# The first four steps of each attention group left to the scheduler, with half a fill tile emitted behind each of them

## The chip, the cores and the metric

The kernel runs on one core of a Trainium2 chip. The metric is device time in microseconds (us) of one execution; several runs of the same kernel are taken and their median is shown. One more execution was recorded by the hardware profiler, and all rows below come from that one.

## The reference, cut to what matters

One layer of a model with width 1024 and 1024 tokens. A projection of x is split into the operands of three branches (sparse attention, spatial gating, mLSTM), and their outputs are gated, merged and normalised. The change touches two places of it: the attention branch, and the projections whose results gate two of the branches.

```python
def query_block(qb):                      # 8 blocks of 128 queries, per group of 4 heads
    s_sel = einsum(q_blk, k_g) - slopes * d_sel       # selected blocks of keys
    p_sel = _masked_softmax(s_sel, m_sel)
    o_sel = einsum(p_sel, v_g)
    s_w = einsum(q_blk, k_w) - slopes * d_w           # window of 256 keys
    p_w = _masked_softmax(s_w, m_w)
    o_w = einsum(p_w, v_w)
o = gates[0] * o_cmp + gates[1] * o_sel + gates[2] * o_win
y_a = o * silu(a_z)
y_b = (gelu(b_u) * mixed) * silu(b_z)
```

## The kernel before, in words

Operands of matmuls are fp32, split into a high and a low part (type fp32r), so that one product is made of three matmuls: `proj_half` (L121) issues 24 matmuls of 128x512 for half a projected tile (8 pieces of the contraction, three products each). A weight tile comes by DMA (`wraw`), ScalarE writes its high part (L90) and VectorE its low part (L91).

Attention works on two groups g of four heads (`attend`, L611). `prep_group` (L359) projects keys and queries into the operands KA/KB and QA/QB. Then come nine steps. Step s does three things for query block s: the row maxima of its window scores (`ps_w`, L487) and selected scores (`ps_s`, L495) in `attn_max`, one VectorE reduction per head and 512 columns (L408, L411), a transpose of these maxima (`ps_m`, L502) and their write into QB (L503). For block s-1 it runs the `Back` object: scores again with the maximum folded into the operand (`ps_st`, L529 and L530), the exponential on ScalarE (L532), the product with V (`ps_o`, L557), four operations on VectorE that add each branch to `o` (L564 to L568), and `finish`, which transposes `o` (`ps_ot`, L574) and copies it into `ya`. For block s+1 it starts the compressed branch, `attn_cmp` (`ps_c` L425, softmax on VectorE and ScalarE, `ps_t` L461, `ps_co` L471).

Each matmul output lies in a bank of PSUM, taken in turn from a pool by name: two banks each for the projections ("pj"), for the scores ("st"), for the small outputs of the maxima and the compressed branch ("m") and for `ps_o`/`ps_ot` ("o").

The order of TensorE within a group is written out by hand: all of `attend` stands inside `tc.manual_schedule(engines={PE})`, so the matmuls of attention keep the order of the text. The other engines' orders are made by the scheduler from the dependences and its own modelled times.

Work that does not depend on attention stands behind it in the text: the fill tiles. `fill_bu` (L592) projects half a tile, then applies GELU into `yb` (its last operation is L173); `fill_bz` (L600) projects half a tile and multiplies `yb` with its SiLU; `fill_az` (L581) does the same for `ya`. Each half is one call of `proj_half` (24 matmuls, L127, output `ps_pj`). The scheduler slips these matmuls between those of attention where it models a wait there. Behind `attend(0)` stand bu and bz of 0 to 2, behind `attend(1)` bu and bz of 3 and az of 0 to 3.

A line number of the kernel after is one higher than before up to L588 (L574 before is L575 after).

Of the kernel before, what the change touches and what calls it, by code (L numbers as in the profile page):

```python
# [2 lines left out]

# [1 line left out]

# [17 lines left out]
NT = T // P  # L23
# [5 lines left out]
HPG = 4  # L29
# [14 lines left out]
def hybrid_kernel(ctx, tc, xm, pT, wfm, wvg, wtm, cmpw1, cmpw2, cpos, vecs, sgwT, sgb,  # L44
# [21 lines left out]
    def pst(tag, bufs, name=None):  # L66
        return ps.tile([P, 512], F32, tag=tag, bufs=bufs, name=name or f"ps_{tag}")

    def pj():
        return pst("pj", 2)  # L70
# [94 lines left out]
    def gelu2(dst, src, n):  # L165

        sq = tp.tile([P, 512], F32, tag="ge_a", bufs=2, name="ge_a")[:, :n]
        if len(src.shape) == 3:
            sq = sq.rearrange("p (a b) -> p a b", a=src.shape[1])
        act(sq, src, AF.Square, scale=GK)  # L170
        stt(out=sq, in0=sq, scalar=1.0, in1=src, op0=OP.add, op1=OP.mult)
        act(sq, sq, AF.Tanh, scale=GC)
        stt(out=dst, in0=sq, scalar=1.0, in1=src, op0=OP.add, op1=OP.mult)  # L173
# [10 lines left out]
    def wf(i, parts=1):  # L184
        return load_w(wfm[i], KT, P, parts)
# [72 lines left out]
    for m in range(4):  # L258
        for r, half in ((0, 0), (0, 1), (1, 0), (1, 1)) if m == 0 else ((0, 0), (1, 0), (0, 1), (1, 1)):
            k = 2 * m + r  # L260
# [52 lines left out]
    for kv in range(2):  # L313
        st = stk[kv]
        ph = pst("m", 2)
        for v in range(2):
            zb = yp.tile([P, T], F32, tag="y", bufs=YB, name="zb")
            z4 = zb[:, 0:1008].rearrange("p (j g n) -> p j g n", j=8, g=2)
            for j in range(8):
                i = 16 * v + 2 * j  # L320
# [40 lines left out]
    def prep_group(g):  # L361
        d = {}
        d["KAs"] = pk.tile([P, T], F32R, tag="KAs", bufs=1, name="KAs")
        d["KBs"] = pk.tile([P, T], F32R, tag="KBs", bufs=1, name="KBs")
        d["KAw"] = pk.tile([P, T], F32R, tag="KAw", bufs=1, name="KAw")
        d["KBw"] = pk.tile([P, T], F32R, tag="KBw", bufs=1, name="KBw")
        for n in "sw":
            vv.tensor_scalar_mul(d["KB" + n][64:128, 0:1], xls[3][1][64:128, 0:1].bitcast(F32), 0.0)
        nc.gpsimd.dma_start(out=d["KBs"][64:128, :], in_=augk[0])
        nc.gpsimd.dma_start(out=d["KBw"][64:128, :], in_=augk[1])  # L370
        w = wf(FM["kw"] + g)
        for half in range(2):
            po = pj()
            proj_half(po, w, half, xh, xl)
            s = slice(half * 512, half * 512 + 512)
            for j, n in enumerate(("s", "w")):
                src = po[j * 64:j * 64 + 64, :]
                A, B = d["KA" + n], d["KB" + n]
                nc.scalar.copy(A[0:64, s], src)
                nc.scalar.copy(B[0:64, s], src)  # L380
                vv.tensor_sub(A[64:128, s], src, B[0:64, s].bitcast(F32))
        QA, QB = [], []
        for hf in range(4):
            qa = pa2.tile([P, 2, HPG, P], F32R, tag="QA", bufs=4, name="QA")
            qb = pa2.tile([P, 2, HPG, P], F32R, tag="QB", bufs=4, name="QB")
            nc.gpsimd.dma_start(out=qb[64:128, :, :, :], in_=augq[g, hf])
            QA.append(qa)
            QB.append(qb)
        for pr in range(2):
            w = wf(FM["q"] + 2 * g + pr)  # L390
            for half in range(2):
                po = pj()
                proj_half(po, w, half, xh, xl)
                for a in range(2):
                    h = 2 * pr + a
                    for b in range(2):
                        src = po[a * 64:a * 64 + 64, b * 256:b * 256 + 256].rearrange("p (b q) -> p b q", b=2)
                        qh = QB[2 * half + b][0:64, :, h, :]
                        nc.scalar.mul(qh, src, 0.125)
                        nc.scalar.mul(QA[2 * half + b][64:128, :, h, :], src, 0.125)  # L400
                        stt(out=QA[2 * half + b][0:64, :, h, :], in0=src, scalar=0.125, in1=qh.bitcast(F32),  # L401
                            op0=OP.mult, op1=OP.subtract)
        d["QA"], d["QB"] = QA, QB
        return d
# [73 lines left out]
    def attn_max(g, qb, d):  # L478

        QB = d["QB"][qb // 2][:, qb % 2]  # L480
        mx = pa2.tile([P, 8], F32, tag="mx", bufs=3, name="mx")
        mx2 = pa2.tile([P, 4], F32, tag="mx2", bufs=3, name="mx2")
        j0 = max(0, qb - 2)
        nw = (qb - j0 + 1) * P
        for h in range(HPG):
            pw = pst("m", 2, "ps_w")
            mm(pw[:, 0:nw], lhsT=QB[:, h, :], rhs=d["KBw"][:, j0 * P:j0 * P + nw], start=True, stop=True)  # L487
            rowmax(mx[:, 4 + h:5 + h], pw, nw, winm[:, 384 - nw:384] if qb >= 2 else zrow[:, 512 - nw:512])
            yield
        ns = (qb + 1) * P  # L490
        for h in range(HPG):
            for c0 in range(0, ns, 512):
                n = min(512, ns - c0)
                pw = pst("m", 2, "ps_s")
                mm(pw[:, 0:n], lhsT=QB[:, h, :], rhs=d["KBs"][:, c0:c0 + n], start=True, stop=True)  # L495
                dst = mx if c0 == 0 else mx2
                rowmax(dst[:, h:h + 1], pw, n, zrow[:, 512 - n:512] if c0 + n == ns else None)
                yield
        if ns > 512:
            vv.tensor_max(mx[:, 0:4], mx[:, 0:4], mx2)  # L500
        pm = pst("m", 2, "ps_m")
        nc.tensor.transpose(pm[0:8, 0:P], mx, ident)  # L502
        vv.tensor_tensor(out=QB[96:104, :, :], in0=pm[0:8, 0:P].unsqueeze(1).to_broadcast([8, 4, P]),  # L503
                         in1=nblk.unsqueeze(2).to_broadcast([8, 4, P]), op=OP.mult)
# [76 lines left out]
    def fill_az(i):  # L581
        w = wf(FM["az"] + i)
        for half in range(2):
            po = pj()
            proj_half(po, w, half, xh, xl)
            y = ya[i][:, half * 512:half * 512 + 512]
            z = tp.tile([P, 512], F32, tag="ge_a", bufs=2, name="zz")
            act(z, po, AF.Tanh, scale=0.5)  # L588
            stt(out=z, in0=z, scalar=1.0, in1=po, op0=OP.add, op1=OP.mult)
            stt(out=y, in0=z, scalar=0.5, in1=y, op0=OP.mult, op1=OP.mult)  # L590

    def fill_bu(i):  # L592
        w = wf(FM["bu"] + i)
        for half in range(2):
            po = pj()
            proj_half(po, w, half, xh, xl)
            gelu2(yb[i][:, half * 512:half * 512 + 512], po, 512)

    def fill_bz(i):
        w = wf(FM["bz"] + i)  # L600
        for half in range(2):
            po = pj()
            proj_half(po, w, half, xh, xl)
            z = tp.tile([P, 512], F32, tag="ge_a", bufs=2, name="zz")
            silu2(z, po, 512, z)
            y = yb[i][:, half * 512:half * 512 + 512]
            vv.tensor_mul(y, y, z)

    def attend(g):  # L611
        with tc.manual_schedule(engines={mybir.EngineType.PE}):
            d = prep_group(g)
            cmp_ = attn_cmp(g, 0, d)
            next(cmp_)
            next(cmp_)
            for step in range(NT + 1):
                back = Back(g, step - 1, d) if step else None
                mxs = attn_max(g, step, d) if step < NT else iter(())
                nmx = (4 + HPG * (1 + step // 4)) if step < NT else 0  # L620
                last = back.n if back else 2
                done = 0
                for k in range(last + 1):
                    upto = nmx * (k + 1) // (last + 1)
                    mid = (done + upto + 1) // 2
                    for _ in range(done, mid):
                        next(mxs)
                    if back and k < back.n:
                        back.scores(k)
                    for _ in range(mid, upto):  # L630
                        next(mxs)
                    done = upto
                    if k == 0:
                        if step < NT:
                            next(cmp_)
                        cmp_ = attn_cmp(g, step + 1, d) if step + 1 < NT else iter(())
                        next(cmp_, None)
                    if back and k:
                        back.values(k - 1)
                if back:  # L640
                    back.finish()
                next(mxs, None)
                next(cmp_, None)
    attend(0)
    for i in range(3):
        fill_bu(i)
        fill_bz(i)
    attend(1)
    fill_bu(3)
    fill_bz(3)  # L650
    for i in range(4):
        fill_az(i)
    if "ya" in dbg:
        for i in range(4):
            nc.sync.dma_start(dbg["ya"][i], ya[i])
# [478 lines left out]
    for tt in range(NT):  # L1134
# [5 lines left out]
        for c in range(npc):  # L1140
            s = slice(c * n, c * n + n)
            pe = pst("m" if tt == 1 else "o", 2, "ps_e")
            i = 0
# [28 lines left out]
        last = tt == NT - 1  # L1172
# [118 lines left out]
```

## Time and profile before

| | us |
|---|---|
| median of 3 runs | 1372.73 |
| lowest and highest of them | 1371.12, 1374.52 |
| the profiled execution | 1371.17 |
| its span in the trace | 1369.1 |
| TensorE busy | 1337.7 (98%) |
| VectorE busy | 844.4 (62%) |
| ScalarE busy | 526.1 (38%) |
| GpSimd busy | 152.8 (11%) |

The span runs from the first to the last instruction that the profiler saw; the profiled execution's own time has 2.1 us around it and lies 1.6 us below the median. PE is TensorE, DVE VectorE, ACT ScalarE, POOL GpSimd. A row of the timeline gives the start and the duration of an instruction (or of a few merged ones, with their count), and in brackets the idle time of the engine just before it with what ended it. Matmuls are pipelined, so that the start-to-start distance, not the duration, is what a matmul takes of the engine.

### The profile page before, as it was taken

To read this page: it belongs to the slowest core of one execution; us is meant where nothing else is said; L and a number is where in the kernel's file an instruction comes from. 1 tells how busy PE (TensorE), PEld (TensorE's weight loads), DVE (VectorE), ACT (ScalarE), POOL (GpSimd) and SP (SyncE) were. 2 spreads that over 40 slices of the span, in tenths; PEclk is the share of its full clock that TensorE was granted. 3 is DMA by queue.
4 is the path that set the end of the run, shared out by engine and by line. 5 is a ranking of instruction groups with operands and counts; after the bars stand their busy time and mean duration, and the time that the engine had idled before them with its cause. 6 is when DMAs were issued, how large, how long until landed. Compare 5 with 4: busy or idle time off the path is not lost.

```text
span 1369.1 us, 18928 instructions
## 1 busy us (share of the span) xinstructions
PE 1337.7 (98%) x7135; PEld 1130.5 (83%) x7135; DVE 844.4 (62%) x1991; ACT 526.1 (38%) x1059; POOL 152.8 (11%) x173
## 2 busy tenths in 40 slices
PE   8998999998999999999999999999999999999997
PEld 6986888886888899988888888888878887888786
DVE  6247777336777467647776678766544555334855
ACT  6354333344333343135455355553442212324211
POOL 0012211101120100001001000010000444000312
PEclk9999999999999999999999999999999999999999
DMA  9131001111002141333223332236346543114201
GB/s 316 32 71 50 24 28 28 38 48 43 9 24 69 41 155 54 132 108 124 82 73 108 108 110 79 81 120 212 108 169 208 194 152 108 47 62 126 105 32 47
DMA packets 48059, 127.46 MB, mean 93 GB/s; under 512 B 5208, under 2 KB 16344, under 8 KB 47968
## 3 DMA queue, kind: packets, MB, share of 16 engines
q1 hardware_dynamic: 47008, 123.11, 27.4%
q0 software_dynamic: 960, 3.15, 1.1%
q8 instruction: 56, 0.92, 0.3%
q14 instruction: 35, 0.29, 0.1%
HBM read 101.00 MB, written 25.23 MB: 92 GB/s over the span
## 4 chain that ended last, share of the span: by engine, by line
PE 90%; DVE 5%; ACT 2%; DMA 2%; issue 1%; SPq 0%; POOL 0%; DVEq 0%; ACTq 0%; POOLq 0%
PE ps_pj L127 19%; PE ps_a L837 14%; PE ps_b L127 9%; PE ps_b L837 8%; PE ps_o L557 7%; PE ps_g L1106 5%; PE ps_st L148 3%; PE ps_pj L148 3%; PE ps_c L837 3%; PE ps_st L529 2%; PE ps_st L530 2%; PE ps_v L136 2%; PE ps_e L1146 2%; PE ps_s L495 1%; PE ps_w L487 1%
## 5 line engine op out<-in xcount | busy, mean ns | idle before, releaser
L127 PE MATMUL ps_pj<-xh,whi 128*128 128x512 f32 x288 | 115.5, 401 | 2.3 <-DVE QA L401 2.3
L127 PE MATMUL ps_pj<-xh,wlo 128*128 128x512 f32 x288 | 115.2, 400 | 0.0
L127 PE MATMUL ps_pj<-xl,whi 128*128 128x512 f32 x288 | 114.6, 398 | 0.0
L557 PEld LDWEIGHTS ps_o<-V,pt 128*128 128x128 f32 x912 | 110.2, 191 | 3.4
L557 PE MATMUL ps_o<-V,pt 128*128 128x65 f32 x912 | 108.3, 271 | 0.0
L532 ACT ACTIVATE pt<-ps_st 128x512 f32<-128x512 f32 x114 | 62.8, 596 | 89.3 <-PE ps_st L530 88.6
L837 PE MATMUL ps_a<-op_lo,sh 128*128 128x512 f32 x240 | 94.1, 392 | 0.0
L837 PE MATMUL ps_a<-op_hi,sl 128*128 128x512 f32 x240 | 93.8, 391 | 0.0
L837 PE MATMUL ps_a<-op_hi,sh 128*128 128x512 f32 x240 | 93.8, 391 | 0.0
L824 DVE TENSOR_TENSOR sl<-ss,sh 128x512 fp32r<-128x512 f32 x80 | 54.8, 690 | 59.0 <-ACT sh L823 58.9
L90 ACT CAST whi<-wraw 128x1024 fp32r<-128x1024 f32 x46 | 48.3, 1049 | 94.8 <-PE ps_b L127 44.7
L127 PE MATMUL ps_b<-sp_hi,wlo 128*128 128x512 f32 x192 | 74.8, 390 | 1.3 <-DVE wlo L91 1.3
L127 PE MATMUL ps_b<-sp_lo,whi 128*128 128x512 f32 x192 | 74.7, 389 | 0.0
L91 DVE TENSOR_TENSOR wlo<-wraw,whi 128x1024 fp32r<-128x1024 f32 x46 | 62.3, 1353 | 19.7 <-ACT whi L90 15.5
L127 PE MATMUL ps_b<-sp_hi,whi 128*128 128x512 f32 x192 | 73.9, 389 | 0.0
L1065 POOL TENSOR_TENSOR M<-M,gt 128x512 f32<-128x512 f32 x32 | 43.8, 1378 | 199.1 <-DVE gt L1064 183.5
L127 PEld LDWEIGHTS ps_pj<-xh,whi 128*128 128x128 f32 x288 | 54.3, 188 | 13.7 <-PE ps_pj L127 3.9
L127 PEld LDWEIGHTS ps_pj<-xh,wlo 128*128 128x128 f32 x288 | 54.3, 188 | 10.0
L127 PEld LDWEIGHTS ps_pj<-xl,whi 128*128 128x128 f32 x288 | 54.3, 189 | 9.3
L823 ACT CAST sh<-mraw 128x512 fp32r<-128x512 f32 x60 | 37.4, 623 | 57.1 <-PE ps_a L837 30.8
L823 ACT CAST sh<-ss 128x512 fp32r<-128x512 f32 x80 | 49.6, 620 | 22.9 <-PE ps_b L837 22.1
L824 DVE TENSOR_TENSOR sl<-mraw,sh 128x512 fp32r<-128x512 f32 x60 | 43.6, 727 | 22.8 <-ACT sh L823 22.8
(369 smaller groups left out, 3534.2 us busy)
## 6 DMA issues: line engine op xcount, KB each, us to landing
mraw<-in_wfm_dram SPq DMA_DIRECT2D x40, 512.0 KB, 3.6
gsc<-gt SPq DMA_DIRECT2D x24, 512.0 KB, 2.6
gt<-gsc SPq DMA_DIRECT2D x24, 512.0 KB, 4.3
wraw<-in_wfm_dram SPq DMA_DIRECT2D x18, 512.0 KB, 3.5
xraw<-in_xm_dram SPq DMA_DIRECT2D x14, 512.0 KB, 5.5
yraw<-ysc SPq DMA_DIRECT2D x12, 512.0 KB, 3.4
wraw<-in_wbr_dram SPq DMA_DIRECT2D x12, 512.0 KB, 5.0
wraw<-in_wtm_dram SPq DMA_DIRECT2D x8, 512.0 KB, 4.0
```

The lines of the kernel that those rows point to most:

```text
L90: nc.scalar.copy(hi[:, c], raw[:, c])
L91: vv.tensor_sub(lo[:, c], raw[:, c], hi[:, c])
L127: mm(po[:M, :], lhsT=a[:, k, :], rhs=b(k, half), start=(i == 0), stop=(i == n - 1))
L136: mm(po[:, :n], lhsT=tok(a, k, tt), rhs=b[:, k % 4, :], start=(i == 0), stop=(i == tot - 1))
L148: mm(po, lhsT=tok(a, 4 * i + k, tt), rhs=b[:, k, :], start=(i == 0 and tt % 2 == 0 and k == 0 and j == 0), stop=(i == 1 and k == 3 and j = ...
L532: act(pt.rearrange("p h q -> p (h q)"), sp, AF.Exp)
L557: mm(po[:, h * 65:h * 65 + 65], lhsT=pt[:, h, :], rhs=V[:, j, vi, :], start=(first and h == 0), stop=last, skip_group_check=True)
L823: nc.scalar.copy(hi, src)
L824: vv.tensor_sub(lo, src, hi)
L837: mm(bank, lhsT=l[a][:, k, :], rhs=r[b], start=first and k == 0 and i == 0, stop=k == K - 1 and i == 2, skip_group_check=True)
L1065: nc.gpsimd.tensor_add(M[n][:, s], M[n][:, s], t[:, s])
L1106: mm(po[:, 0:n], lhsT=a[k][:, ts_], rhs=b[k][:, s], start=(k == 0 and i == 0), stop=(k == KT - 1 and i == 2))
```

## The change

`FREE = 4`: `prep_group` and steps 0 to 3 of each group stand outside `manual_schedule`, so that the scheduler orders their matmuls on TensorE too; steps 4 to 8 stay inside. The three fill functions become generators that yield after each half, and one half is emitted behind each free step: bu0 and bz0 in group 0, bu3 and bz3 in group 1. The other fills stand behind the groups as before. No operation is added or taken away.

```diff
     def fill_bu(i):
         w = wf(FM["bu"] + i)
...
             proj_half(po, w, half, xh, xl)
             gelu2(yb[i][:, half * 512:half * 512 + 512], po, 512)
+            yield
...
-    def attend(g):
+    FREE = 4
+
+    def attend(g, fills):
+        d = prep_group(g)
+        cmp_ = attn_cmp(g, 0, d)
+        next(cmp_)
+        next(cmp_)
+
+        def one(step):
+            nonlocal cmp_
...
+        for step in range(FREE):
+            one(step)
+            next(fills, None)
         with tc.manual_schedule(engines={mybir.EngineType.PE}):
-            d = prep_group(g)
...
+            for step in range(FREE, NT + 1):
+                one(step)
+
+    attend(0, chain(fill_bu(0), fill_bz(0)))
+    for _ in chain(fill_bu(1), fill_bz(1), fill_bu(2), fill_bz(2)):
+        pass
+    attend(1, chain(fill_bu(3), fill_bz(3)))
+    for _ in chain(*(fill_az(i) for i in range(4))):
+        pass
-    attend(0)
-    for i in range(3):
-        fill_bu(i)
-        fill_bz(i)
-    attend(1)
-    fill_bu(3)
-    fill_bz(3)
-    for i in range(4):
-        fill_az(i)
```

The body of `one(step)` is that of the loop before, word for word. What it does to the order is seen where step 1 of group 0 ends and step 2 begins. On TensorE, before, the last `ps_o` of block 0 is followed at once by the transposes of `o` (here `q_1095` and `kbd_201` are numbered buffers of the compressed branch):

```order
L425 MATMUL ps_c<-kbd_201,q_1095 128x128 x2
L127 MATMUL ps_pj<-xl,whi 128x512
L495 MATMUL ps_s<-KBs,QB 128x256 x4
L557 MATMUL ps_o<-V,pt 128x65 x8
L574 MATMUL ps_ot<-ident,o 128x128 x2
L502 MATMUL ps_m<-ident,mx 8x128
L461 MATMUL ps_t<-ident,pcm 128x128 x2
L487 MATMUL ps_w<-KBw,QB 128x384
```

After the change the same place on TensorE begins so (the last `ps_o` is the fourth row):

```order
L472 MATMUL ps_co<-vbd_203,pts 128x128 x2
L426 MATMUL ps_c<-kbd_201,q_1129 128x128 x2
L558 MATMUL ps_o<-V,pt 128x65 x2
L496 MATMUL ps_s<-KBs,QB 128x256
L558 MATMUL ps_o<-V,pt 128x65 x6
L530 MATMUL ps_st<-QA,KAw 128x512
L496 MATMUL ps_s<-KBs,QB 128x256
L530 MATMUL ps_st<-QA,KAw 128x512
L496 MATMUL ps_s<-KBs,QB 128x256
```

and after fifteen matmuls of a fill tile, the last `ps_s` and the transpose `ps_m`, goes on with:

```order
L462 MATMUL ps_t<-ident,pcm 128x128 x2
L128 MATMUL ps_pj<-xh,whi 128x512
L128 MATMUL ps_pj<-xh,wlo 128x512
L128 MATMUL ps_pj<-xl,whi 128x512
L488 MATMUL ps_w<-KBw,QB 128x384
L128 MATMUL ps_pj<-xh,whi 128x512
L531 MATMUL ps_st<-QB,KBw 128x512 x2
L575 MATMUL ps_ot<-ident,o 128x128
L488 MATMUL ps_w<-KBw,QB 128x384
```

The transposes `ps_ot` have moved behind 19 matmuls of a fill tile and behind the first `ps_w` of step 2; two `ps_st` of step 2 that need no maximum (those with QA) have moved ahead.

On VectorE, before, the same place reads (the low part of a weight stands between the two branches of `o`):

```order
L436 TENSOR_TENSOR pcm<-pcm,sm 128x256
L568 SCALAR_TENSOR_TENSOR o<-ps_o,osc,o 128x64 x4
L566 TENSOR_TENSOR osc<-osc,gates 128x4
L91 TENSOR_TENSOR wlo<-wraw,whi 128x1024
L568 SCALAR_TENSOR_TENSOR o<-ps_o,osc,o 128x64 x4
L503 TENSOR_TENSOR QB<-ps_m,nblk 8x512
L173 SCALAR_TENSOR_TENSOR yb<-ge_a,ps_pj 128x512
```

After, a `yb` of a fill stands ahead of it (six rows higher than the first row here), the write of QB ahead of the second branch of `o`, and `wlo` behind two row maxima:

```order
L569 SCALAR_TENSOR_TENSOR o<-ps_o,osc,o 128x64 x2
L567 TENSOR_TENSOR osc<-osc,gates 128x4
L504 TENSOR_TENSOR QB<-ps_m,nblk 8x512
L569 SCALAR_TENSOR_TENSOR o<-ps_o,osc,o 128x64 x4
L412 ISA junk,mx<-ps_w,cr 128x384
L412 ISA mx 128x1
L578 COPY ya<-ps_ot 128x128
L412 ISA junk,mx<-ps_w,cr 128x384
L412 ISA mx 128x1
L92 TENSOR_TENSOR wlo<-wraw,whi 128x1024
```

Over the attention of each group, TensorE passes 74 times from an fp32 matmul (transposes, `ps_o`, `ps_c`, `ps_co`) to an fp32r one, before it did so 66 times. From the free steps' end on, the order on TensorE is that of before.

## Rows read from the trace of the kernel before

**Rows 1.** The page, part 1: busy time of each engine, with share and instructions.

```profile
PE 1337.7 (98%) x7135; PEld 1130.5 (83%) x7135; DVE 844.4 (62%) x1991; ACT 526.1 (38%) x1059; POOL 152.8 (11%) x173
```

**Rows 2.** Windows: stretch and length in us, busy PE, PEld, DVE, ACT, POOL; PEclk, DMA, GB/s.

```profile
98.00:120.00 22.00, 20.63 (x109) 15.83 (x107) 15.35 (x57) 12.76 (x42) 5.61 (x8) 1.00 0.16 43
120.00:128.00 8.00, 4.40 (x18) 3.29 (x17) 6.25 (x24) 2.08 (x6) 0.00 (x0) 0.57 0.23 66
128.00:304.00 176.00, 175.93 (x1038) 151.14 (x1037) 106.03 (x343) 64.46 (x152) 24.29 (x38) 1.00 0.11 32
334.20:342.20 8.00, 4.40 (x17) 3.28 (x17) 6.28 (x24) 2.02 (x6) 0.00 (x0) 0.61 0.20 67
342.20:593.00 250.80, 250.80 (x1756) 229.77 (x1756) 165.67 (x491) 82.86 (x169) 21.95 (x34) 1.00 0.22 70
```

**Rows 3.** Waits of PE, 90 to 180 us: waited for; total, times, longest in us.

```profile
PE ps_ot L574 <- DVE o L568: 3.3, 1, 3.3
PE ps_pj L127 <- DVE QA L401: 1.2, 2, 0.6
PE ps_s L495 <- DVE mx L411: 0.6, 2, 0.3
```

**Rows 4.** Timeline of PE, group 0, end of step 1.

```profile
118.57 1.90 PE L557 MATMUL ps_o<-V,pt 128*128 128x65 f32 x16
123.71 0.77 PE L574 MATMUL ps_ot<-ident,o 128*128 128x128 f32 x2 [3.25 <-DVE o L568]
...
125.47 0.69 PE L487 MATMUL ps_w<-KBw,QB 128*128 128x384 f32 x1 [0.35 <-DVE QB L503]
...
127.66 0.39 PE L487 MATMUL ps_w<-KBw,QB 128*128 128x384 f32 x1
```

**Rows 5.** Timeline of DVE, the same place.

```profile
121.12 0.85 DVE L568 SCALAR_TENSOR_TENSOR o<-ps_o,osc,o 128x64 f32<-128x64 f32 x4
...
121.96 1.22 DVE L91 TENSOR_TENSOR wlo<-wraw,whi 128x1024 fp32r<-128x1024 f32 x1
123.10 0.85 DVE L568 SCALAR_TENSOR_TENSOR o<-ps_o,osc,o 128x64 f32<-128x64 f32 x4
124.73 0.68 DVE L503 TENSOR_TENSOR QB<-ps_m,nblk 8x512 fp32r<-8x512 f32 x1 [0.78 <-PE ps_m L502]
125.45 0.69 DVE L173 SCALAR_TENSOR_TENSOR yb<-ge_a,ps_pj 128x512 f32<-128x512 f32 x1
```

**Rows 6.** Timeline of PE, group 1, the same place.

```profile
337.93 0.77 PE L574 MATMUL ps_ot<-ident,o 128*128 128x128 f32 x2 [3.25 <-DVE o L568]
...
341.88 0.52 PE L487 MATMUL ps_w<-KBw,QB 128*128 128x384 f32 x1
...
342.85 0.48 PE L127 MATMUL ps_pj<-xh,whi 128*128 128x512 f32 x1
```

**Rows 7.** Timeline of PE, group 0, later steps: the same work without a wait.

```profile
140.55 0.44 PE L487 MATMUL ps_w<-KBw,QB 128*128 128x384 f32 x1
...
141.75 0.33 PE L487 MATMUL ps_w<-KBw,QB 128*128 128x384 f32 x1
...
142.29 0.47 PE L127 MATMUL ps_pj<-xl,whi 128*128 128x512 f32 x1
...
157.19 0.27 PE L574 MATMUL ps_ot<-ident,o 128*128 128x128 f32 x1
157.30 0.27 PE L502 MATMUL ps_m<-ident,mx 128*8 128x128 f32 x1
...
157.55 0.48 PE L127 MATMUL ps_pj<-xh,whi 128*128 128x512 f32 x1
```

**Rows 8.** Timeline of PE: three fill matmuls behind a ps_o, the first one wider spaced.

```profile
136.14 0.48 PE L127 MATMUL ps_pj<-xh,wlo 128*128 128x512 f32 x1
136.46 0.39 PE L127 MATMUL ps_pj<-xl,whi 128*128 128x512 f32 x1
136.69 0.40 PE L127 MATMUL ps_pj<-xh,whi 128*128 128x512 f32 x1
```

More of the change, by code (lines that the diff above doesn't have):

```diff
@@ L2 @@
 from contextlib import ExitStack
+from itertools import chain
 import numpy as np
@@ L597, in fill_bu @@
             gelu2(yb[i][:, half * 512:half * 512 + 512], po, 512)
+            yield
     def fill_bz(i):
@@ L607, in fill_bz @@
             vv.tensor_mul(y, y, z)
-    def attend(g):
-        with tc.manual_schedule(engines={mybir.EngineType.PE}):
-            d = prep_group(g)
[L614 to L643, printed above, removed]
@@ L644, in hybrid_kernel @@
-    attend(0)
-    for i in range(3):
-        fill_bu(i)
-        fill_bz(i)
-    attend(1)
-    fill_bu(3)
-    fill_bz(3)
-    for i in range(4):
-        fill_az(i)
+            yield
+    FREE = 4
[6 more added lines that the diff above has]
+            nonlocal cmp_
+            back = Back(g, step - 1, d) if step else None
+            mxs = attn_max(g, step, d) if step < NT else iter(())
+            nmx = (4 + HPG * (1 + step // 4)) if step < NT else 0
+            last = back.n if back else 2
+            done = 0
+            for k in range(last + 1):
+                upto = nmx * (k + 1) // (last + 1)
+                mid = (done + upto + 1) // 2
+                for _ in range(done, mid):
+                    next(mxs)
+                if back and k < back.n:
+                    back.scores(k)
+                for _ in range(mid, upto):
+                    next(mxs)
+                done = upto
+                if k == 0:
+                    if step < NT:
+                        next(cmp_)
+                    cmp_ = attn_cmp(g, step + 1, d) if step + 1 < NT else iter(())
+                    next(cmp_, None)
+                if back and k:
+                    back.values(k - 1)
+            if back:
+                back.finish()
+            next(mxs, None)
+            next(cmp_, None)
+        for step in range(FREE):
+            one(step)
+            next(fills, None)
+        with tc.manual_schedule(engines={mybir.EngineType.PE}):
+            for step in range(FREE, NT + 1):
+                one(step)
```

## The prediction

> **What bounds the kernel now.** I read the page's first part before anything else: TensorE (PE) is busy for 98% of the span, the next engine (VectorE, DVE) for 62% [rows 1]. So a change in order can win only where PE is idle or runs at a low clock, and I look for those places with the windows over the two attention groups. The reader is to see two kinds of stretch there [rows 2]. From 128 to 304 us PE is busy for 175.93 of 176 us, from 342.2 to 593 us for all of 250.8, both at a granted clock of 1.00: nothing to win. From 120 to 128 us and from 334.2 to 342.2 us it is busy for 4.40 of 8 us, and the granted clock is 0.57 and 0.61, between the two levels of 1.00 (2.4 GHz) and 0.5 (1.2 GHz). Ahead of the first of these, from 98 to 120 us, lie 22.00 - 20.63 = 1.37 us of idle time at clock 1.00, in short pieces.
>
> The list of what PE waits for names the cause [rows 3]: one wait of 3.3 us of the transposes `ps_ot` for `o`, two of 0.6 us for QA, two of 0.3 us for a row maximum. The timelines show how the long one comes about [rows 4, 5]. The last `ps_o` of block 0 ends at 118.57 + 1.90 = 120.47 us. DVE then does the first branch of `o` (0.85 us), a weight's low part (1.22 us) and the second branch (0.85 us), which is done at 123.95 us. All that time PE has the transposes at the head of its hand-made order and can't pass them. Then the maxima are transposed, DVE writes QB (0.68 us), and the first `ps_w` of step 2 starts at 125.47 us. What follows is at half speed: from that `ps_w` over four `ps_st` to the next it takes 127.66 - 125.47 = 2.19 us, and the same six matmuls in a later step 141.75 - 140.55 = 1.20 us [rows 4, 7]. Group 1 has the same wait of 3.25 us in the same place [rows 6].
>
> **The change, part by part.**
>
> *The hole is filled.* After the change 19 fill matmuls, `ps_t` and two `ps_st` stand between the last `ps_o` and the transposes. A fill matmul takes 136.69 - 136.46 = 0.23 us from start to start [rows 8], so 19 are 4.4 us: about as long as DVE needs for `o` and QB. The stretch from 120.47 to 125.47 us, 5.00 us, holds useful work that takes little at full clock: 157.30 - 157.19 = 0.11 us for each of the two `ps_ot`, and 157.55 - 157.30 = 0.25 for `ps_m` and the two `ps_t` behind it [rows 7], together 0.47. What can be won is 5.00 - 0.47 = 4.53 us in each group. Nothing is made shorter by this: 19 fill matmuls that stood later now stand here, and since PE is full from 128 us on, the whole rest moves forward by as much.
>
> *The clock.* If PE doesn't stop, it doesn't fall to the lower level, and 2.19 - 1.20 = 0.99 us are won per group [rows 4, 7]. In group 1 the slow stretch goes on a little: from the second `ps_w` to the first fill matmul 342.85 - 341.88 = 0.97 us, against 142.29 - 141.75 = 0.54 [rows 6, 7], 0.43 more. Hole and clock together: 2 x (4.53 + 0.99) + 0.43 = 11.5 us. By the Trainium skill, "TensorE: Matmul & The Clock Gate", section "Terms", a stretch at the lower level costs its length times one minus the level's share of the full clock; a mean of 0.57 over 8 us would then cost 3.4 us a group in place of my 0.99, and the gain would be some 5 us larger. The trace speaks for the smaller figure, since most of the slow stretch was idle and only 18 matmuls stood in it.
>
> *The short waits.* In step 0 two `ps_st` that need no maximum move ahead, and fill matmuls are free to stand between `ps_s`. I count one of the two waits for QA (half of 1.2) and one of the two for a maximum (half of 0.6) as gone [rows 3]: 0.9 us a group, 1.8 in all. The first wait for QA, in `prep_group`, stays, as no filler is ready.
>
> *More changes of operand type.* In each group 8 more fp32r matmuls follow an fp32 one. The first fill matmul behind `ps_o` takes 136.46 - 136.14 = 0.32 us to the next start, those behind it 0.23 [rows 8]: 0.09 us each, so 2 x 8 x 0.09 = 1.4 us lost, all of it on PE and so on the path.
>
> *New short waits.* The fill halves bring their own work for DVE and ScalarE into steps 1 to 3: `yb` (0.69 us), a weight's low part (1.22 us) [rows 5]. DVE was busy for 15.35 of 22 us from 98 to 120 us [rows 2], and with two or three more such operations in each step it comes near to full, so that some `ps_s` or `ps_w` will find their bank still being read. The trace doesn't show this mixture. From below: nothing, as in later steps of the same shape with fill work (128 to 304 us, 0.07 us idle) [rows 2]. From above: idle time as in 98 to 120 us, 1.37 us in 22 us, over the two steps that follow, some 29 us (to 157 us): 1.8 us a group. I take 0.75 a group, nearer the lower end, because fill matmuls can stand in these steps as they do after 128 us: 1.5 us lost.
>
> *Costed at nothing.* DMAs: the next weights are asked for at about the same place; PE's order from step 4 on is the old one, and the fills that were moved forward are missing nowhere, since the totals are equal and enough of them lie behind each group. Were a weight tile late in step 1, PE would wait as long as DVE and ScalarE need for its two parts, some 2 us. POOL and ACT are busy for 11% and 38% [rows 1], and their orders hardly change.
>
> The sum: 11.5 + 1.8 - 1.4 - 1.5 = 10.4 us faster. The profiled execution took 1371.17 us, 1.6 below the median of 1372.73; 1360.8 by its own time is **1362.3 us** by the median. About 0.3% (4.1 us) is what a measurement of this kernel can tell from no change.
>
> **The rivals.**
>
> *The hole comes back in smaller pieces.* DVE stays the slow side: `wlo`, 1.22 us, and `yb`, 0.69 us, now stand between row maxima in step 2 or 3 [rows 5], where PE has only two "m" banks and runs out of what it may do. For it: DVE at 70% before any of this is added [rows 2]. Against: fill matmuls that need no "m" bank are at hand. Price: the upper end of the short waits (1.8 a group) and one such operation of 1.2 us waited for in full: 2 x (1.8 + 1.2) - 1.5 = 4.5 us less gain, 1366.8 us.
>
> *The clock still falls, and more often: slower.* One wait of 3.25 us becomes many short ones spread over four steps, and PE is given the lower clock in them. Price: by the window at 0.57 [rows 2] each us of such a stretch in which PE is busy loses 0.43 us. The gain of 10.4 is gone if 10.4 / 0.86 = 12 us in each group run so, and 17 us (14.5 / 0.86) make it slower by 0.3%. With 25 us, less than half of the free steps, it would be 1362.3 + 21.5 = 1384 us. Against it: from 98 to 120 us PE has 1.37 us of short idle times and keeps 1.00 [rows 2]. By the Trainium skill, the same page, section "A second HAM failure mode: psum-queue depth-cycling", short idle times between groups of matmuls that cycle through PSUM banks make the clock swing; by that rule this rival would be the likely one. The trace so far disagrees, with short waits, none above 0.6 us [rows 3], at 1.00.
>
> *The fill isn't there in time.* The scheduler goes by modelled times; if the fill's bank or weight comes late on the chip, PE stands before `ps_pj` as it stood before `ps_ot`, and the kernel takes between 1369 and 1374 us. For it: in group 0 the third half waited for a bank which the `yb` operation behind QB frees (L173 at 125.45 us) [rows 5]. Against: after the change that operation stands ahead of `o`.
>
> **How the numbers follow.** Forecast as summed: 0.72. Smaller pieces: 0.16. Fill late, about no change: 0.07. Clock falls: 0.05. The most that the rows allow is all idle time of 98 to 128 us and the like in group 1, 2 x (1.37 + 3.60) = 9.9 us, and the 4.40 busy us of each slow window [rows 2] halved, 4.4: 14.3 us, 1358.4. If the waits for QA in `prep_group` went too (half of 1.2 a group) [rows 3], it would be 1357.2; I put the end at 1357.5. At the other end stand the smaller pieces with one us more of waits: 1368.0. Faster by over 0.3% means below 1368.6: the first two cases but for some of the second, 0.87; within 0.3% 0.08; slower 0.05, the clock.
>
> **What would show it.** Right: no wait of 3 us before `ps_ot`; a clock of 1.00 in all windows from 98 to 304 us and in group 1; less than 2 us of idle PE between 98 and 160 us; the work behind attention some 10 us earlier at equal busy time. Transition cost: PE's busy time up by about 1.4 us, less what the clock gives back. Wrong: waits of over 1 us for `mx`, `o`, QB or `wlo` in steps 2 and 3 (smaller pieces), a wait of `ps_pj` for a bank or a weight (fill late), or a clock under 1.00 between 90 and 160 us. A gain of 10 us in attention that isn't in the total would mean that something behind attention, such as a load, had waited there all along.

## The result, and the profile after

| | before | after |
|---|---|---|
| median | 1372.63 (4 runs) | 1357.64 (4 runs, 1357.20 to 1358.08) |
| ratio, 95% interval | | 0.989 (0.9873 to 0.9907) |
| profiled execution | 1371.17 | 1358.08 |
| its span | 1369.1 | 1356.0 |

The change made the kernel 15.0 us faster by the medians. The forecast was 1362.3 us, 10.4 us faster; the measured time lies 0.14 us inside the lower end of the range (1357.5 us).

The page's first part of the profile after, to be read beside [rows 1]: TensorE (PE) has 4.8 us less of busy time for the same 7135 instructions.

```profile
PE 1332.9 (98%) x7135; PEld 1127.8 (83%) x7135; DVE 840.9 (62%) x1993; ACT 526.1 (39%) x1057; POOL 152.2 (11%) x173
```

The windows after, to be read beside [rows 2] (the later stretches are shifted by what was won ahead of them). The columns are the stretch and its length, busy PE, PEld, DVE, ACT and POOL, the granted clock, the DMA share and GB/s.

```profile
98.00:120.00 22.00, 21.05 (x113) 16.13 (x113) 14.54 (x51) 11.95 (x34) 5.61 (x8) 1.00 0.13 39
120.00:128.00 8.00, 8.00 (x43) 6.44 (x43) 7.01 (x32) 3.76 (x13) 0.64 (x1) 1.00 0.03 10
128.00:300.00 172.00, 171.85 (x1018) 148.21 (x1017) 106.05 (x344) 65.07 (x155) 23.79 (x37) 1.00 0.13 37
327.40:335.40 8.00, 8.00 (x45) 6.47 (x43) 7.10 (x32) 3.76 (x13) 0.64 (x1) 1.00 0.02 7
```

Both holes are gone: PE is busy for 8.00 of 8 us in each, at 1.00 in place of 0.57 and 0.61. The first window has 0.95 us of idle time in place of 1.37.

What PE waits for after, 60 to 180 us (total, times, longest), to be read beside [rows 3]:

```profile
PE ps_pj L128 <- DVE QA L402: 0.6, 1, 0.6
PE ps_t L462 <- DVE pcm L437: 0.5, 1, 0.5
PE ps_s L496 <- DVE mx L412: 0.3, 1, 0.3
```

The wait of `ps_ot` is gone, with one wait for QA, one for a maximum and the short one of `ps_w` for QB [rows 4]; a wait of `ps_t` for the compressed branch's softmax is new. The place of the hole, in the timeline of PE after, to be read beside [rows 4]:

```profile
118.26 1.45 PE L558 MATMUL ps_o<-V,pt 128*128 128x65 f32 x12
...
120.18 0.28 PE L496 MATMUL ps_s<-KBs,QB 128*128 128x256 f32 x1
120.30 0.40 PE L128 MATMUL ps_pj<-xh,whi 128*128 128x512 f32 x1
...
124.95 0.36 PE L488 MATMUL ps_w<-KBw,QB 128*128 128x384 f32 x1
...
125.85 0.27 PE L575 MATMUL ps_ot<-ident,o 128*128 128x128 f32 x1
125.88 0.42 PE L488 MATMUL ps_w<-KBw,QB 128*128 128x384 f32 x1
```

The transposes start 2.1 us later than before (125.85 against 123.71), and that costs nothing, since fill work stands in front of them.

Where the time came from is seen between two marks that both kernels pass: the first `ps_c` of group 0, and the first projection behind attention (`ps_pj<-whi,xh`). Between them lies the same work. A tile's rows, of before and then of after, give the first and last start of a group of instructions in us:

```profile
L425 PE MATMUL ps_c<-kbd,q x4: 270/274/275, 98.3 to 98.6; 128*128 128x128 f32 x4
L148 PE MATMUL ps_pj<-whi,xh x2: 277/280/283, 493.3 to 493.6; 128*128 128x256 f32 x2
```

```profile
L426 PE MATMUL ps_c<-kbd,q x4: 270/274/275, 98.7 to 99.1; 128*128 128x128 f32 x4
L149 PE MATMUL ps_pj<-whi,xh x24: 277/283/283, 479.7 to 493.7; 128*128 128x256 f32 x24
```

Attention with its fills took 493.3 - 98.3 = 395.0 us before and 479.7 - 98.7 = 381.0 after: 14.0 us less. I call this the attention stretch below; it leaves out what happens at the start and behind attention, which turned out to matter in the experiments. It matters here too: the whole spans of these two profiles differ by 1369.1 - 1356.0 = 13.1 us only, since the kernel after took 0.5 us more ahead of this stretch and 0.5 us more behind it.

### The profile page after: what moved, and what is told of

The parts are those of the page before. It is cut to its first block, busy times and chain, and to the rows that moved or that the text cites. A ratio compares the mean times of both kernels' runs of the same rounds, so it can differ in the third digit from the quotient of the medians.

```text
span 1356.0 us, 18923 instructions
## 1 busy us (share of the span) xinstructions
PE 1332.9 (98%) x7135; PEld 1127.8 (83%) x7135; DVE 840.9 (62%) x1993; ACT 526.1 (39%) x1057; POOL 152.2 (11%) x173
## 4 chain that ended last, share of the span: by engine, by line
PE 89%; DVE 5%; ACT 3%; DMA 2%; issue 1%; SPq 0%; POOL 0%; DVEq 0%; ACTq 0%; POOLq 0%
PE ps_pj L128 19%; PE ps_a L849 14%; PE ps_b L128 9%; PE ps_b L849 8%; PE ps_o L558 7%; PE ps_g L1118 5%; PE ps_st L149 3%; PE ps_pj L149 3%; PE ps_c L849 3%; PE ps_st L530 2%; PE ps_st L531 2%; PE ps_v L137 2%; PE ps_e L1158 2%; PE ps_s L496 1%; PE ps_w L488 1%
```

## The experiments

### The two halves of the change, each alone

The change does two things: it frees the order of attention's matmuls, and it moves half fills to between the steps. The first experiment keeps the freedom and puts the fills back behind the groups:

```diff
-    attend(0, chain(fill_bu(0), fill_bz(0)))
-    for _ in chain(fill_bu(1), fill_bz(1), fill_bu(2), fill_bz(2)):
+    attend(0, iter(()))
+    for _ in chain(*(f(i) for i in range(3) for f in (fill_bu, fill_bz))):
...
```

> Steps 0 to 3 free as in the change, but no half fill between them (all fills behind the groups, as before). In the order of TensorE three fill matmuls (before none, after the change 19) and some scores of step 2 stand between the last ps_o of block 0 and the first ps_ot. Theory 'hole' (the gain is that fill matmuls cover the wait of ps_ot for o, and with it the fall of the clock): covered are some 1.5 to 2.5 us of each hole of 4.5, and the clock may or may not fall: 1363 to 1368 us. Rival 'freedom' (the scheduler's own order of attention is the better one, whatever the fills do): the whole gain, 1357 to 1359 us. Rival 'place of the fills' (only their place in the text counts, since it sets the order on VectorE too): no gain, 1371 to 1374 us.

The second keeps the order by hand in each step and leaves the half fills between the steps (`prep_group` stands in a hand-made stretch too):

```diff
         for step in range(FREE):
-            one(step)
+            with tc.manual_schedule(engines={mybir.EngineType.PE}):
+                one(step)
             next(fills, None)
```

> Each of steps 0 to 3 in its own hand-made stretch (order of attention as before), the half fills between them as in the change. 11 fill matmuls, 2.5 us, stand ahead of the first ps_ot. Theory 'hole': 2.5 of 4.5 us covered in each group, and the clock kept if the rest of the wait is short: 1363 to 1368 us, with a wait of ps_ot for o of 0.7 to 2 us left. Rival 'freedom': no gain, 1371 to 1374 us. Rival 'place of the fills': the whole gain, 1357 to 1359 us.

Measured: freedom alone 1366.52 us (ratio 0.9958, 0.9946 to 0.9971), half fills alone 1361.29 us (0.9919, 0.9906 to 0.9933). Freedom alone is where the theory of the hole put it, half fills alone are 1.7 us better than that; neither alone is the whole, and neither is nothing. The windows at the hole, freedom alone and then half fills alone:

```profile
120.00:128.00 8.00, 6.48 (x34) 5.31 (x33) 5.89 (x22) 4.79 (x10) 1.97 (x4) 0.79 0.02 5
```

```profile
120.00:128.00 8.00, 8.00 (x48) 6.67 (x47) 6.38 (x28) 2.71 (x12) 0.00 (x0) 1.00 0.22 67
```

With freedom alone the hole is only broken up (waits of 1.1 us for the softmax and of 0.5 for its copy), and in this profile the clock still falls. With half fills alone it is closed: eleven fill matmuls and a VectorE order in which `o` comes earlier (its second branch starts 3.2 us behind the first `ps_o`, before 4.5) were enough. The expectation had a wait of 0.7 to 2 us left over there; none was. The attention stretch is 479.6 - 97.8 = 381.8 us with half fills alone, and 485.9 - 98.0 = 387.9 with freedom alone. So the place of the fills carries 13.2 of the 14.0 us in attention; freedom adds 0.8 on top of it, and is worth 7.1 alone. These are single profiles. That of freedom alone is the longest of its five runs (1369.88 us, with a mean granted clock of 0.993 where the others have 0.995 to 0.998), so in the others the clock fell less, and freedom alone was probably worth more there. By the medians the two are 6.1 and 11.3 us faster than before.

### Why half fills alone vary

The profiled execution of that kernel, 1358.2 us, was its shortest; the others took 1360.3 to 1362.6. It was run once more:

> The kernel with the order by hand and half fills between (e2_halves_only) once more, for a second profile: its profiled execution, 1358.2 us with the clock at 1.00, was the shortest of five (the others 1360.3 to 1362.6). Theory 'clock': what is left of the waits at the hole makes the clock fall in the longer ones, seen as a window below 1.00 behind the first ps_ot. Rival: the clock stays and the difference lies elsewhere (start, loads).

This time 1363.62 us. The attention stretch is the same, 480.1 - 98.4 = 381.7 us, and clocked at 1.00. The part behind it took 1361.5 - 480.1 = 881.4 us, in the first profile 1356.1 - 479.6 = 876.5. So the theory of the clock falls as to the place. The timeline of PE there:

```profile
508.15 0.35 PE L149 MATMUL ps_pj<-whi,xh 128*128 128x256 f32 x1 [1.95 <-DVE vb L174]
...
509.43 0.41 PE L149 MATMUL ps_pj<-wlo,xh 128*128 128x256 f32 x1
509.64 0.41 PE L149 MATMUL ps_pj<-whi,xl 128*128 128x256 f32 x1
```

and the window of it:

```profile
508.00:512.00 4.00, 3.85 (x20) 3.88 (x21) 4.00 (x6) 2.07 (x4) 0.00 (x0) 0.57 0.02 7
```

A projection behind attention waits for a PSUM bank that VectorE has not read yet, and behind that wait the matmuls stand 0.21 us apart in place of 0.12: the clock fell. In the first profile the same wait was 0.9 us and the clock stayed. Neither the kernel before nor the change has such a wait in its profile.

The clock fell in a second place too, and there the two profiles have the same idle time. Both have one wait of 1.2 us there, of `ps_a` for ScalarE's `sh`, as all profiles of this case do. The window of it, first profile and then second:

```profile
576.00:596.00 20.00, 18.53 (x103) 15.89 (x102) 9.20 (x14) 7.29 (x13) 0.00 (x0) 1.00 0.44 119
576.00:596.00 20.00, 18.53 (x108) 16.22 (x107) 6.58 (x11) 6.21 (x11) 0.00 (x0) 0.91 0.46 133
```

So the same kernel, with the same idle time in the same place, kept the clock in one execution and lost it in another. The longer runs have lower mean clocks on record (0.996 and 0.997, against 0.998 for the shortest), which fits such falls in them.

### The hole made shorter

The third experiment leaves the order of PE as it was before and lets ScalarE copy a fill's result out of PSUM at once, which moves the weight's low part out of the place between the two branches of `o`:

```diff
             proj_half(po, w, half, xh, xl)
+            if i in (0, 3):
+                y = yb[i][:, half * 512:half * 512 + 512]
+                nc.scalar.copy(y, po)
+                po = y
             gelu2(yb[i][:, half * 512:half * 512 + 512], po, 512)
```

> The kernel before, with one more copy by ScalarE in bu0 and bu3: the projection's result is copied out of PSUM at once, and GELU works from the copy, so that the bank comes free early. TensorE's order is that of before (no fill matmul in the hole); on VectorE the low part of the weight (1.22 us) no longer stands between the two branches of o. Theory 'hole': the wait of ps_ot falls from 3.25 to about 2.0 us, the gain is 2 x 1.2 = 2.4 us, and up to 4 more if the clock no longer falls: 1366 to 1370.5 us. Rival 'the bank alone held the fill back': fill matmuls would cover the hole, 1358 to 1362 us; the order speaks against it. Rival 'VectorE's order does not matter': 1372 to 1374 us.

Measured: 1376.17 us, 3.6 slower than before (ratio 1.0029, 1.0017 to 1.004). The expectation failed in its result, not in its first step: the wait fell to 2.3 us. Two of the waits of PE over the whole span, and the window of the hole:

```profile
PE ps_ot L574 <- DVE o L568: 4.5, 2, 2.3
PE ps_pj L148 <- DVE zz L589: 3.5, 1, 3.5
```

```profile
120.00:128.00 8.00, 5.38 (x21) 4.22 (x20) 6.33 (x27) 4.29 (x10) 0.46 (x1) 0.57 0.21 66
```

The clock is 0.57 in that window as before, with 5.38 us of matmuls in it in place of 4.40 [rows 2]: more work runs slowly, and of 2 us less of waiting the attention stretch (492.6 - 98.1 = 394.5 us) keeps 0.5. And a wait of 3.5 us for the last fill's bank came up behind attention, as in the run above, with a fall of the clock behind it (0.83 from 496 to 506 us). The part behind attention took 1374.1 - 492.6 = 881.5 us, before 1369.1 - 493.3 = 875.8: the kernel lost its time there.

### Where the freedom has to be

> FREE = 2 in place of 4: only steps 0 and 1 free, with two half fills (bu0, bu3); the other two halves stand behind the group. Theory 'hole': the hole lies in step 1, steps 2 and 3 had no idle time before, so the gain is that of the change within 1.5 us: 1356.5 to 1359 us. Rival 'freedom': steps 2 and 3 give their share, so about half of the gain, 1363 to 1367 us.

Measured: 1358.16 us (0.9896, 0.9883 to 0.991), attention stretch 479.6 - 98.3 = 381.3. Two free steps do what four do.

> FREE = 9: no hand-made stretch at all, half fills behind the first four steps. Theory 'hole' (steps 4 to 8 had no idle time left): the same as the change within 1.5 us, 1356.5 to 1359 us; small new waits could make it slower by up to 3. Rival 'freedom' (the scheduler's order is better wherever it is allowed): steps 4 to 8 add to the gain, 1350 to 1356 us. Rival 'hand order is needed where VectorE is the slower side': 1361 us or more.

Measured: 1361.34 us (0.9925, 0.9911 to 0.9938), slower than the change by 3.7. In attention next to nothing is won (480.8 - 100.2 = 380.6 us). The largest wait of PE is again the one behind attention:

```profile
PE ps_pj L149 <- DVE zz L590: 2.9, 1, 2.9
```

So the order by hand costs nothing from step 4 on. Of the 3.6 us by which its profile is longer than that of the change, 2.6 lie behind attention, where the last fills end. Another 1.5 us were lost ahead of attention (its first `ps_c` starts at 100.2 us in place of 98.7), where the clock fell in this profile:

```profile
14.00:18.00 4.00, 4.00 (x12) 2.84 (x11) 3.83 (x4) 3.32 (x4) 0.00 (x0) 0.57 1.03 397
```

In the profile of the change the clock is 1.00 there. Whether the order of the later steps has to do with that fall isn't shown.

### The clock alone

Thirteen matmuls whose result is never read stand in the hole of the kernel before:

```diff
+                if step == 1:
+                    dm = pst("st", 2, "ps_dm")
+                    for i in range(13):
+                        mm(dm, lhsT=d["KAw"][:, 0:P], rhs=back.QA, start=(i == 0), stop=(i == 12))
                 if back:
                     back.finish()
```

> The kernel before, with 13 additional matmuls of 128x512 by hand between the last ps_o of block 0 and the first ps_ot in each group (13 x 0.23 = 3.0 us into a free bank of the scores, their result never read). The wait of ps_ot for o stays as it is for the rest of the kernel, but TensorE works through it; this prices the clock alone. Theory 'clock' (the slow stretch behind the hole costs half of the TensorE time in it): in the trace before, 3.7 us of matmuls lie at the lower level behind each hole, so 1.85 us a group come back: 1368 to 1369.5 us. Rival 'the price of the prediction' (0.99 a group, 0.43 more in group 1): 1370 us. Rival 'the hole is all' (the clock costs nothing of its own): 1372 to 1374 us.

Measured: 1367.99 us, 4.1 faster than before on the same chip (0.9971, 0.9961 to 0.9982). More work made the kernel faster. In the window of the hole the clock is 1.00; in the timeline of PE the wait is filled, and from the first `ps_w` behind it to the second it takes 126.91 - 125.70 = 1.21 us, where before it took 2.19 [rows 4]:

```profile
120.00:128.00 8.00, 7.19 (x40) 5.63 (x39) 7.08 (x28) 2.79 (x9) 0.14 (x1) 1.00 0.23 67
120.71 3.24 PE L643 MATMUL ps_dm<-QA,KAw 128*128 128x512 f32 x13
124.15 0.62 PE L574 MATMUL ps_ot<-ident,o 128*128 128x128 f32 x2 [0.21 <-DVE o L568]
...
125.70 0.45 PE L487 MATMUL ps_w<-KBw,QB 128*128 128x384 f32 x1 [0.60 <-ACT pts L463]
...
126.91 0.33 PE L487 MATMUL ps_w<-KBw,QB 128*128 128x384 f32 x1
```

The attention stretch is 490.5 - 98.7 = 391.8 us, 3.2 less. That is 1.6 us a group by the trace and 2.05 by the medians, on both sides of the 1.85 of the theory; the prediction's price, 2.4 us for both groups, was too small for the clock taken by itself.

### The price of a change of operand type

```diff
+                split = step > FREE and k > 0 and k < back.n
+                if split:
+                    back.scores(k, slice(0, 1))
+                    for _ in range(mid, upto):
+                        next(mxs)
+                    back.values(k - 1, slice(None, 1))
+                    back.scores(k, slice(1, 2))
+                    back.values(k - 1, slice(1, 2))
+                    done = upto
+                    continue
```

> The changed kernel, with the second score tile and the row maxima of steps 5 to 8 placed between the two tiles of ps_o, so that 28 more fp32r matmuls follow an fp32 one (176 in place of 148 from the first ps_c to the last ps_ot); nothing is added or removed. It prices the change of operand type. By the prediction, 0.09 us each: 2.5 us slower than the change, 1360.2 us. Rival 'the switch is free': the gap behind the first fp32r matmul is 0.09 us longer, but the last ps_o gives way after 0.083 us in place of 0.17: within 0.7 us of the change, 1357 to 1358.3 us. A wait of a row maximum or of a score would show as idle time of TensorE and is to be taken off.

Measured: 1359.36 us (0.9911, 0.9897 to 0.9924), 1.7 above the change. But the profile has a wait behind attention that the change lacks,

```profile
PE ps_pj L149 <- DVE vb L174: 1.1, 1, 1.1
```

and in the attention stretch, where all 28 switches lie, 479.5 - 98.1 = 381.4 us stand against 381.0: 0.4 / 28 = 0.015 us each. A switch is nearly free, not 0.09 (a net price: what the new order may have won elsewhere is in it).

### The kernel before and the change once more, and a better version

> The kernel before, unchanged, for a second profile. The first one was taken from the shortest of its runs (1371.17 us, median 1372.6), so part of the measured gain may lie in something that this profile does not show. If the clock falls in one place more in longer runs, its windows show a granted clock below 1.00 outside of 120 to 128 and 334 to 342 us; otherwise the extra time is idle time, at the start or at the loads behind attention.

It came out at 1371.31 us, again at the lower end of the runs of before (1370.6 to 1375.0 in all runs shown), with the same two holes and, up to 1360 us, no other window below 1.00. What the longer runs do is not seen in a profile.

The eighth kernel takes away the wait for QA in `prep_group`:

```diff
-                po = pj()
+                po = pst("st", 2, "ps_q") if pr else pj()
```

> The changed kernel, with the last two query projections of each group in the banks of the scores, which stand empty at that time, in place of the two banks of the projections. What is left of idle time there is one wait of 0.65 us a group for QA, that is for a bank. Theory (the bank alone makes this wait): both waits go, 1.3 us less, 1356 to 1357 us. Rival (the time is filled by something else that PE then waits for, the q2 of the compressed branch above all): the same as the change.

> The changed kernel once more, on the same chip as the run before, to compare the two directly and for a second profile: 1357 to 1358.5 us, clock 1.00 in all windows of attention.

Measured on one chip: 1355.50 us with the other banks (0.9875, 0.986 to 0.9889), 1357.19 for the change (0.9886, 0.987 to 0.9903). The two intervals overlap in their comparison with before, but no run of the new version (1354.47 to 1357.08) is above the median of the change: a gain of 1.7 us is likely, though small. Its window ahead of attention, of the new version and then of the change:

```profile
78.00:98.00 20.00, 20.00 (x92) 16.65 (x91) 7.94 (x17) 11.36 (x30) 1.71 (x3) 1.00 0.18 53
```

```profile
78.00:98.00 20.00, 19.35 (x86) 15.62 (x85) 8.00 (x15) 10.97 (x27) 1.46 (x2) 1.00 0.20 55
```

The 0.65 us are gone, as expected: the wait was one for a bank.

## Why the prediction was right, and which of its terms were off

The mechanism was the right one: fill matmuls cover the wait of `ps_ot`, and the clock no longer falls. The size was less so. Two terms were off by 1 to 2 us each, both to the low side, and the time fell inside the range by 0.14 us only; in that, luck had a part. Its terms, against the 14.0 us of the attention stretch:

**The hole** (4.53 us a group): no run measures it alone, but the gain in its place (below) leaves no room for much less. With eleven or nineteen fill matmuls in front, PE is busy for all 8 us of the window. By one reading it was too small: the prediction let it begin where the last `ps_o` is shown to end, at 120.47 us. That `ps_o` starts at 120.19 us, and where nothing is waited for the next matmul starts 0.08 us behind a last `ps_o`, so the hole began at 120.27: 0.2 us a group more.

**The clock** (2.4 us in both groups): 3.2 us in the trace and 4.1 by the medians when it was taken out alone. The prediction priced only the six matmuls from `ps_w` to `ps_w` and, in group 1, what follows them; the slow rows ahead of them (`ps_ot`, `ps_m`, `ps_t`) were put to the hole. From `ps_ot` to `ps_w` it took 125.47 - 123.71 = 1.76 us, and 125.70 - 124.15 = 1.55 with the clock kept. So 0.2 us a group of the difference was counted, under another name. By the Trainium skill, "TensorE: Matmul & The Clock Gate", section "Terms", the two windows at 0.57 and 0.61 would have cost an estimated 3.4 and 3.1 us; the run shows less, as part of the slow stretch was idle. The "some 5 us larger" that the prediction gives for that dearer clock is 4.5 by its own figures.

**The short waits** (1.8 us): this is the term that failed most. The prediction took them from the list of waits, as 0.3 us for a maximum in each group. That list counts only time in which no matmul is shown busy. In the timeline of before, four `ps_s` of step 1:

```profile
116.86 0.28 PE L495 MATMUL ps_s<-KBs,QB 128*128 128x256 f32 x1
117.30 0.76 PE L495 MATMUL ps_s<-KBs,QB 128*128 128x256 f32 x2 [0.16 <-DVE pcm L427]
118.34 0.39 PE L495 MATMUL ps_s<-KBs,QB 128*128 128x256 f32 x1 [0.28 <-DVE mx L411]
118.57 0.67 PE L557 MATMUL ps_o<-V,pt 128*128 128x65 f32 x5
```

From the first start to the start of `ps_o` are 118.57 - 116.86 = 1.71 us, though each of these matmuls lets the next one start after 0.12 us where nothing is waited for: 120.18 to 120.30 in the timeline after. So they lose 1.71 - 4 x 0.12 = 1.2 us, and the list names 0.16 + 0.28 = 0.44. With fill matmuls and `ps_st` between the `ps_s` these waits went, 2 x (1.23 - 0.3) = 1.9 us more in both groups than predicted.

**The switches** (1.4 us lost): wrong. The prediction saw that the first fp32r matmul behind an fp32 one takes 0.32 us to the next start in place of 0.23, and did not look at the other side: the last `ps_o` of a row lets the next matmul start after 0.08 us, another `ps_o` only after 0.11 (the 0.17 that the expectation of the switches gives for it isn't in the trace). That is a third of the 0.09. Measured by itself, a switch costs 0.015 us net, 0.2 us for the 16 that the change adds; where the rest comes back isn't shown. 1.2 us too much was taken off.

**The new short waits** (1.5 us lost) and the gone wait for QA: they came, but in step 0, ahead of the place where they were expected: `ps_t` waits 0.5 us for the softmax. In steps 2 and 3 there is none: PE is idle for nothing between 128 and 160 us.

How much of it lies where can be read from the starts of `ps_m`, the transpose that ends a step's maxima. Before:

```profile
111.86 0.28 PE L502 MATMUL ps_m<-ident,mx 128*8 128x128 f32 x1
...
139.45 0.27 PE L502 MATMUL ps_m<-ident,mx 128*8 128x128 f32 x1
```

and after:

```profile
113.06 0.27 PE L503 MATMUL ps_m<-ident,mx 128*8 128x128 f32 x1
...
137.62 0.27 PE L503 MATMUL ps_m<-ident,mx 128*8 128x128 f32 x1
```

From step 0's to step 2's are 27.59 us before, with 28 fill matmuls in between, and 24.56 us after, with 46 of them. At 0.227 us each (twenty in a row take 4.54 us before, from 99.39 to 103.93 us), the attention work of these two steps took 21.2 us before and 14.1 after: 7.1 us less in this one place of group 0, against 5.5 predicted for hole and clock there. Step 0, from the first `ps_c`, took 0.7 us more. With 0.4 us less in step 3 the sum is 6.8 us, and 7.1 for group 1 by the same count.

So: 10.4 us predicted, 0.4 more for the hole, 1.9 for the short waits, 1.2 for the switches, and some 0.4 us less for the waits of step 0 and 3 together: 13.5, against 14.0 in the trace. The other 0.5 us, part of it perhaps the clock's, isn't assigned. The medians differ by 15.0, the two pairs of profiles by 13.1 and 14.2 us of span; both profiles of before fell on its shorter runs. So some 1 to 2 us are shown by no profile. They stay open; the longer runs of another kernel differed behind attention.

The rivals: smaller pieces of the hole did not come back; the clock did not swing in attention, though short waits of 0.3 to 0.6 us stay; and but for the wait for QA ahead of attention no `ps_pj` of the two groups waited for a bank or a weight. The trace thus does not bear out here what the Trainium skill says of short idle times between groups of matmuls (same page, "A second HAM failure mode: psum-queue depth-cycling"): in the windows of the change the clock is 1.00 throughout. One sign was of little use, PE's busy time: the prediction had it rise by 1.4 us for the switches, less what the clock gives back (its 2.4 us); it fell by 4.8, and since the end of a matmul on the page is modelled, waits that are shown as busy went with it.

## What to carry to other kernels

Work that is to cover a wait should stand near that wait in the text: here the place of the fills gave most of the gain, and freedom of the order without it less than half by the medians. Count a wait on a pipelined engine from start to start, against the distance of the same instructions elsewhere, not from the list of waits; a matmul that is shown busy may be waiting already. After any change of order look at the seam behind the changed part: here the last fill's bank cost waits of between nothing and 3.5 us there, and in some runs the clock behind them, enough to turn a gain around.

## What was not expected of the hardware

Useless work paid: thirteen unread matmuls in each of two waits of 3.25 us made the kernel 4.1 us faster, since the clock stayed at its upper level (2.4 GHz) behind them. And the length of a wait alone did not decide whether the clock fell: behind the 1.2 us of `ps_a` it fell in one execution and stayed in another of the same kernel; behind 1.95 us it fell to its lower level in one run (matmuls 0.21 us apart), behind 2.88 us in another kernel it did not (0.12 us apart in the timeline of the kernel with all steps free):

```profile
486.70 0.39 PE L149 MATMUL ps_pj<-whi,xh 128*128 128x256 f32 x1 [2.88 <-DVE zz L590]
486.92 0.28 PE L149 MATMUL ps_pj<-wlo,xh 128*128 128x256 f32 x1
487.04 0.28 PE L149 MATMUL ps_pj<-whi,xl 128*128 128x256 f32 x1
487.16 0.28 PE L149 MATMUL ps_pj<-whi,xh 128*128 128x256 f32 x1
```
